# Windowed matmul on one core: row blocks of decreasing size, and PSUM sums added several banks at a time

## The chip, the cores and the metric

The kernel runs on one core of a Trainium2 chip. The metric is the device time of one execution in microseconds (us); the median of ten executions before the change is 182.23 us (181.94 to 182.52).

## The reference

```
B, S, D, W = 4, 4096, 4096, 64
x: [B, S, D] float32    w: [D, D] float32    offsets: [B] int64
for b in range(B):
    o = int(offsets[b])
    results.append(x[b, o:o+W] @ w)
return np.stack(results)          # [4, 64, 4096] float32
```

Four windows of 64 rows are cut out of x at offsets that are known only at run time, and each is multiplied by the same matrix w. Put together, the windows are 256 rows, so the work is one product of 256 x 4096 by 4096 x 4096. The matrix w is 67 MB of float32 and is read once.

## The kernel before

**Tiles.** The 256 rows are two groups g of 128 rows (two windows each). The contraction runs over 32 k tiles of 128 rows of w. The 4096 output columns are eight pieces c of 512, and two halves ng of 2048: the left half is ng = 0, the right one ng = 1. For each k tile there are 2 x 8 matmuls of 128x512, 512 in all. A matmul's stationary operand is a 128x128 piece of the transposed x, its moving operand 512 columns of w in fp16, and its output one PSUM bank of 512 float32. PSUM has eight banks (`ps[0]` to `ps[7]`, L54). Sums over k are kept in PSUM within a block and added to `acc[g]` in SBUF (float32, 128x4096 for each group) after it.

**Weights.** All of w but the first k tile comes by transfers that POOL issues and that convert float32 to fp16 on the way. K tiles 0 and 1 have tiles of their own. From k tile 2 on, `blocks` (L35) lists a first k tile and r, the number of rows of w that each partition takes: one transfer per block, r x 16 KB of source per partition in one run (L87 to L94). A block of r rows per partition covers r k tiles, and which rows of w belong to which k tile follows the stride r; `x_cols` (L120) picks the matching columns of x. K tiles 24 to 31 are the tail (`k_tail`, L36): they are loaded by column halves, the right half first (`order = [1, 0]`), in transfers of two k tiles by 2048 columns (1 MB as fp16), the last ones of the left half smaller (L97 to L118).

**Buffers.** Blocks and tail use one pool of three buffers, each of 4 x 4096 fp16 per partition (L42). There are eight uses: six blocks, the right half of the tail, the left half of the tail. The fourth use waits until the first is read, and so on. POOL issues in program order, so each transfer waits for the one before it and for its buffer.

**Order of the work.** The order is written out by hand (`manual_schedule`, L56): every engine takes its instructions in the order of the program. First come the transposes of x (L127 to L141), then k tiles 0 and 1, whose sums are copied to `acc` (L169, L171). Then come the blocks in `whole_rows` (L158): for each group and each column piece, one bank takes the r matmuls of the block, and VectorE adds the bank to `acc` (`add_out`, L154). The bank number goes round all eight. The last block (k tiles 21 to 23) is treated in two parts. Its left half goes through `whole_rows` (L178). Its right half is summed in the same PSUM banks as the tail's right half: L193 to L196 run over 11 k tiles on the outside, the two groups and the four column pieces on the inside, so that all eight banks (4 g + j) are open at once. After that VectorE adds two banks of each group, ScalarE copies the other two to `tmp` (L200), VectorE adds `tmp` (L205), and POOL issues the store of the right half of each group (L206, 1 MB each). At last comes the left half of the tail: k tiles 24 to 29 for all eight banks, then k tiles 30 and 31 for two column pieces of each group and then for the other two (L215 to L220). VectorE adds each bank, and the store of each group and each 1024 columns is issued on ScalarE's queue for group 0 and on SyncE's for group 1 (L225).

Of the kernel before, what the change touches and what calls it, by code (L numbers as in the profile page):

```python
# [10 lines left out]
def kernel(  # L11
# [7 lines left out]
    nc = tc.nc  # L19
    fp32 = mybir.dt.float32  # L20
    fp16 = mybir.dt.float16

    B, S, D = x.shape
    _, N = w.shape
    WIN = out.shape[1]
    P = 128
    NT = 512
    NG = N // 2
    n_k = D // P
    n_sub = NG // NT  # L30
    G = B // 2
    POOL = mybir.EngineType.Pool


    blocks = [(0, 1), (1, 1), (2, 4), (6, 4), (10, 4), (14, 4), (18, 3), (21, 3)]  # L35
    k_tail = 24  # L36
    n_fine = 2
    R_MAX = 4

# [2 lines left out]
    wc_pool = ctx.enter_context(tc.tile_pool(name="wc", bufs=3))  # L42
    w1_pool = ctx.enter_context(tc.tile_pool(name="w1", bufs=1))
    acc_pool = ctx.enter_context(tc.tile_pool(name="acc", bufs=1))
    psum_pool = ctx.enter_context(tc.tile_pool(name="ps", bufs=1, space=bass.MemoryType.PSUM))
# [3 lines left out]
    x16 = [x_pool.tile([P, D], fp16, name=f"xrow{g}") for g in range(G)]  # L49
    xT = [x_pool.tile([P, D], fp16, name=f"xT{g}") for g in range(G)]  # L50
    w_one = [w1_pool.tile([P, N], fp16, name=f"w1_{i}") for i in range(2)]
    tmp = [acc_pool.tile([P, NT], fp32, name=f"tmp{i}") for i in range(4)]
    acc = [acc_pool.tile([P, N], fp32, name=f"acc{g}") for g in range(G)]
    ps = [psum_pool.tile([P, NT], fp32, name=f"bank{t}") for t in range(8)]  # L54

    ctx.enter_context(tc.manual_schedule())  # L56

# [10 lines left out]
    for b in range(B):  # L68
        g, m = divmod(b, 2)
# [8 lines left out]
            out=x16[g][m * WIN : (m + 1) * WIN, :],  # L78
            in_=x[b][bass.ds(o, WIN), :],
# [3 lines left out]
    src = {  # L83
        0: lambda a, e: w_one[0][:, a:e],
        1: lambda a, e: w_one[1][:, a:e],
    }
    for k0, r in blocks[2:]:  # L87
        t = wc_pool.tile([P, R_MAX * N], fp16, name="wc", tag="wc")
        nc.gpsimd.dma_start(  # L89
            out=t[:, : r * N],  # L90
            in_=w[k0 * P : (k0 + r) * P, :].rearrange("(p r) n -> p (r n)", r=r),
        )
        for q in range(r):
            src[k0 + q] = lambda a, e, t=t, c=q * N: t[:, c + a : c + e]  # L94


    tail = {}  # L97
    order = [1, 0]
    steps = [(ki, 2, 0, NG) for ki in range(k_tail, n_k, 2)]
    fine_steps = steps[: -(n_fine // 2)]  # L100
    fine_steps.append((n_k - n_fine, n_fine, 0, NG // 2))
    fine_steps += [(ki, 1, NG // 2, NG) for ki in range(n_k - n_fine, n_k)]
    for ng, st in zip(order, (steps, fine_steps)):
        t = wc_pool.tile([P, R_MAX * N], fp16, name="wc", tag="wc")
        pos = 0
        for ki, n, c0, c1 in st:
            wd = c1 - c0
            nc.gpsimd.dma_start(  # L108
                out=t[:, pos : pos + n * wd].rearrange("p (t n) -> p t n", t=n),
                in_=w[ki * P : (ki + n) * P, ng * NG + c0 : ng * NG + c1].rearrange(  # L110
                    "(t p) n -> p t n", p=P
                ),
            )
            for q in range(n):
                for j in range(wd // NT):
                    a = pos + q * wd + j * NT
                    tail[(ki + q, (ng * NG + c0) // NT + j)] = t[:, a : a + NT]
            pos += n * wd  # L118

    def x_cols(g, kt):  # L120
        for k0, r in blocks:
            if k0 <= kt < k0 + r:
                a = k0 * P + kt - k0
                return x16[g][:, a : a + r * (P - 1) + 1 : r]
        return x16[g][:, kt * P : (kt + 1) * P]

    for g in range(G):  # L127
        for t in range(8):
            for i in range(4):
                nc.tensor.matmul(  # L130
                    out=ps[t][:, i * P : (i + 1) * P],
                    lhsT=x_cols(g, 4 * t + i),
                    rhs=identity[:],
                    start=True,
                    stop=True,
                )
            dst = xT[g][:, t * NT : (t + 1) * NT]
            if t % 2 == 0:
                nc.vector.tensor_copy(out=dst, in_=ps[t][:])  # L139
            else:  # L140
                nc.scalar.copy(out=dst, in_=ps[t][:])  # L141

    def mm(bank, g, kt, rhs, start, stop):
        nc.tensor.matmul(  # L144
            out=ps[bank][:],
            lhsT=xT[g][:, kt * P : (kt + 1) * P],
            rhs=rhs,
            start=start,
            stop=stop,
        )  # L150

    def add_out(bank, g, c):
        dst = acc[g][:, c * NT : (c + 1) * NT]
        nc.vector.tensor_add(out=dst, in0=dst, in1=ps[bank][:])  # L154

    n_bank = 0

    def whole_rows(kts, cols, first):  # L158
        nonlocal n_bank
        for g in range(G):  # L160
            for c in cols:
                bank = n_bank % 8
                n_bank += 1
                for i, kt in enumerate(kts):
                    mm(bank, g, kt, src[kt](c * NT, (c + 1) * NT), i == 0, i == len(kts) - 1)
                if not first:
                    add_out(bank, g, c)
                elif c % 2 == 0:
                    nc.vector.tensor_copy(out=acc[g][:, c * NT : (c + 1) * NT], in_=ps[bank][:])  # L169
                else:  # L170
                    nc.scalar.copy(out=acc[g][:, c * NT : (c + 1) * NT], in_=ps[bank][:])  # L171

    whole_rows([0, 1], range(8), True)
    for k0, r in blocks[2:-1]:
        whole_rows(range(k0, k0 + r), range(8), False)
    k0, r = blocks[-1]
    last_block = range(k0, k0 + r)
    whole_rows(last_block, range(order[1] * n_sub, (order[1] + 1) * n_sub), False)  # L178

    def tail_mm(ki, g, ng, j, start, stop):  # L180
        c = ng * n_sub + j
        rhs = src[ki](c * NT, (c + 1) * NT) if ki < k_tail else tail[(ki, c)]
        mm(4 * g + j, g, ki, rhs, start, stop)
# [3 lines left out]
    def store(eng, g, c0, c1, cuts=(0, P)):  # L187
        for a, e in zip(cuts, cuts[1:]):
            eng.dma_start(out=out_rows[g * P + a : g * P + e, c0:c1], in_=acc[g][a:e, c0:c1])  # L189

    ng = order[0]
    kts = list(last_block) + list(range(k_tail, n_k))
    for ki in kts:  # L193
        for g in range(G):
            for j in range(n_sub):
                tail_mm(ki, g, ng, j, ki == kts[0], ki == kts[-1])  # L196
    for g in range(G):
        for j in range(0, n_sub, 2):
            add_out(4 * g + j, g, ng * n_sub + j)
            nc.scalar.copy(out=tmp[2 * g + j // 2][:], in_=ps[4 * g + j + 1][:])  # L200
    for g in range(G):
        for j in range(1, n_sub, 2):
            c = ng * n_sub + j
            dst = acc[g][:, c * NT : (c + 1) * NT]
            nc.vector.tensor_add(out=dst, in0=dst, in1=tmp[2 * g + j // 2][:])  # L205
        store(nc.gpsimd, g, ng * NG, (ng + 1) * NG)  # L206

    ng = order[1]
# [5 lines left out]
    q = [nc.scalar, nc.sync]  # L214
    for h in range(2):  # L215
        js = range(h * n_sub // 2, (h + 1) * n_sub // 2)
        for ki in range(k_fine, n_k):
            for g in range(G):
                for j in js:
                    tail_mm(ki, g, ng, j, False, ki == n_k - 1)  # L220
        for g in range(G):
            for j in js:
                add_out(4 * g + j, g, ng * n_sub + j)
            c0 = ng * NG + h * NG // 2
            store(q[g], g, c0, c0 + NG // 2)  # L225

# [29 lines left out]
```

## Time and profile before

| what | value |
| --- | --- |
| median of ten executions | 182.23 us (181.94 to 182.52) |
| profiled execution, its time | 182.19 us |
| profiled execution, its span | 180.4 us |
| mean granted TensorE clock | 0.912 |
| PE busy | 126.0 us (70%), 576 matmuls |
| VectorE busy | 80.1 us (44%) |
| ScalarE, POOL busy | 16.2 us, 14.5 us |
| weight and store transfers issued by POOL | 36.70 MB, 93.9% of the 16 DMA engines' span |
| read from HBM, written to HBM | 71.30 MB, 4.19 MB |

The profile is of one execution. Its span is the time from the first to the last recorded event, and the execution's own time is 1.8 us more. PE is TensorE (PEld its weight loads), DVE is VectorE, ACT is ScalarE, POOL is GpSimd, SP is SyncE; L154 is line 154 of the kernel. Sizes of transfers are counted as they are written, so the weights count half of what is read for them. The rows by slice cut the span into 40 equal parts of 4.5 us and give the busy share of each in tenths. The chain of waits is followed back from the last instruction to what released it. In a row of a group the first number after the bar is its total busy time in us, the second the mean of one in ns, and behind the next bar stands the idle time of the engine ahead of it and what ended most of it.

### The profile page before, as it was taken

The numbers are of one execution on the slowest core, as the hardware profiler recorded it, in microseconds if no ns is written. First come the engines' busy times: TensorE is split into PE (matmuls) and PEld (weight loads), VectorE is DVE, ScalarE is ACT, GpSimd is POOL, SyncE is SP. The second block draws the span as 40 slices with busy tenths as digits, with TensorE's granted clock in tenths as the row PEclk, the third lists the DMA queues.
The fourth block names the chain that finished last, engine by engine and source line by source line (L and its number), as shares of the span: only waits on it lengthen the run. The fifth ranks groups of instructions, "written<-read, shape, count | busy, mean of one in ns | idle before, by whom it ended". The sixth has DMA issues, their size and how long they took to land.

```text
span 180.4 us, 1505 instructions
## 1 busy us (share of the span) xinstructions
PE 126.0 (70%) x576; PEld 57.0 (32%) x576; DVE 80.1 (44%) x120; ACT 16.2 (9%) x23; POOL 14.5 (8%) x29
## 2 busy tenths in 40 slices
PE   0000789104999199938998599999299999997900
PEld 0000754001444034402443144444134444443400
DVE  0000678100777147831687168899365000640460
ACT  2412556200000000000000000000000000400000
POOL 4600000000000100010001000050501100020000
PEclk9999999955899969985899699999969999999995
DMA  5999979999998899999989989898899999999995
GB/s 182 320 254 214 287 167 203 236 233 225 233 233 189 174 225 233 234 222 233 203 182 211 251 185 251 189 245 191 182 214 217 215 212 214 216 215 206 368 417 206
DMA packets 4952, 40.98 MB, mean 227 GB/s; under 512 B 466, under 2 KB 466, under 8 KB 3282
## 3 DMA queue, kind: packets, MB, share of 16 engines
q0 software_dynamic: 4080, 36.70, 93.9%
q1 hardware_dynamic: 432, 2.10, 3.1%
q10 hardware_dynamic: 434, 2.10, 2.9%
q8 instruction: 4, 0.07, 0.1%
q14 instruction: 2, 0.02, 0.0%
HBM read 71.30 MB, written 4.19 MB: 419 GB/s over the span
## 4 chain that ended last, share of the span: by engine, by line
DMA 63%; PE 26%; issue 3%; DVE 2%; POOL 1%; POOLq 1%; DVEq 0%
DMA wc<-in_w_dram 63%; PE bank L144 26%; DVE acc L154 2%; POOL wc L108 1%; POOLq L70 1%; POOL xrow L77 0%; DVEq L251 0%; POOL identity masks.py:197 0%; POOLq L77 0%; POOL w L66 0%; POOLq masks.py:199 0%; DVEq L154 0%; POOLq L240 0%
## 5 line engine op out<-in xcount | busy, mean ns | idle before, releaser
L144 PE MATMUL bank<-wc,xT 128*128 128x512 f16 x480 | 113.6, 401 | 25.9 <-DMA wc<-in_w_dram 25.9
L154 DVE TENSOR_TENSOR acc<-acc,bank 128x512 f32<-128x512 f32 x100 | 67.1, 687 | 72.2 <-PE bank L144 71.4
L144 PEld LDWEIGHTS <-xT 128*128 128x128 f16 x512 | 51.9, 102 | 94.2 <-DMA wc<-in_w_dram 27.0
L130 PE MATMUL bank<-identity,xrow 128*128 128x128 f16 x64 | 5.5, 264 | 19.8 <-DMA xrow<-in_x_dram 19.8
L139 DVE CAST xT<-bank 128x512 f16<-128x512 f32 x8 | 5.3, 687 | 21.0 <-PE bank L130 21.0
L200 ACT COPY tmp<-bank 128x512 f32<-128x512 f32 x4 | 2.1, 600 | 122.2 <-PE bank L144 122.2
L130 PEld LDWEIGHTS <-xrow 128*128 128x128 f16 x64 | 5.1, 125 | 20.0 <-issue 20.0
L89 POOL DMA_DIRECT2D wc<-in_w_dram x6 | 3.2, 542 | 89.2 <-PE bank L144 89.2
L108 POOL DMA_DIRECT2D wc<-in_w_dram x10 | 6.7, 683 | 34.9 <-PE bank L144 25.3
L144 PE MATMUL bank<-w,xT 128*128 128x512 f16 x32 | 7.1, 379 | 0.0
L169 DVE COPY acc<-bank 128x512 f32<-128x512 f32 x8 | 5.4, 689 | 0.9 <-PE bank L144 0.6
L141 ACT CAST xT<-bank 128x512 f16<-128x512 f32 x8 | 4.4, 592 | 7.1 <-PE bank L130 7.1
L171 ACT COPY acc<-bank 128x512 f32<-128x512 f32 x8 | 4.7, 585 | 2.1 <-PE bank L144 2.1
L189 POOL DMA_DIRECT2D out_dram<-acc x2 | 1.1, 534 | 18.6 <-DVE acc L205 18.6
L205 DVE TENSOR_TENSOR acc<-acc,tmp 128x512 f32<-128x512 f32 x4 | 2.5, 684 | 0.0
L63 ACT CAST w<-acc 128x2048 f16<-128x2048 f32 x1 | 1.9, 1897 | 4.8 <-DMA acc<-in_w_dram 4.8
L77 POOL DMA_DIRECT2D xrow<-in_x_dram x4 | 2.1, 523 | 2.1 <-issue 2.1
L62 ACT CAST w<-acc 128x2048 f16<-128x2048 f32 x1 | 1.9, 1897 | 2.9 <-DMA acc<-in_w_dram 2.9
L62 ACT ACT_TABLE_LOAD x1 | 1.3, 1283 | 1.8 <-PEq L240 1.8
L66 POOL DMA_DIRECT2D w<-in_w_dram x1 | 0.7, 660 | 0.8 <-POOLq L240 0.8
masks.py:199 POOL TENSOR_SCALAR_AFFINE_SELECT identity<-identity 128x128 f16<-128x128 f16 x1 | 0.3, 287 | 0.1
masks.py:197 POOL MEMSET identity<- 128x128 f16 x1 | 0.2, 223 | 0.0
(4 smaller groups left out, 0.4 us busy)
## 6 DMA issues: line engine op xcount, KB each, us to landing
wc<-in_w_dram POOLq DMA_DIRECT2D x4, 4096.0 KB, 48.7
wc<-in_w_dram POOLq DMA_DIRECT2D x7, 1024.0 KB, 27.4
wc<-in_w_dram POOLq DMA_DIRECT2D x2, 3072.0 KB, 34.4
xrow<-in_x_dram POOLq DMA_DIRECT2D x4, 512.0 KB, 14.5
out_dram<-acc POOLq DMA_DIRECT2D x2, 1024.0 KB, 13.9
acc<-in_w_dram SPq DMA_DIRECT2D x1, 1024.0 KB, 5.1
w<-in_w_dram POOLq DMA_DIRECT2D x1, 1024.0 KB, 12.0
acc<-in_w_dram ACTq DMA_DIRECT2D x1, 1024.0 KB, 11.3
```

Of the source, the lines that this page charges most:

```text
L62: nc.scalar.copy(out=w_one[0][:, :NG], in_=w0_32[:, :NG])
L77: nc.gpsimd.dma_start(out=x16[g][m * WIN : (m + 1) * WIN, :], in_=x[b][bass.ds(o, WIN), :],)
L89: nc.gpsimd.dma_start(out=t[:, : r * N], in_=w[k0 * P : (k0 + r) * P, :].rearrange("(p r) n -> p (r n)", r=r),)
L108: nc.gpsimd.dma_start(out=t[:, pos : pos + n * wd].rearrange("p (t n) -> p t n", t=n), in_=w[ki * P : (ki + n) * P, ng * NG + c0 : ng * NG ...
L130: nc.tensor.matmul(out=ps[t][:, i * P : (i + 1) * P], lhsT=x_cols(g, 4 * t + i), rhs=identity[:], start=True, stop=True,)
L139: nc.vector.tensor_copy(out=dst, in_=ps[t][:])
L141: nc.scalar.copy(out=dst, in_=ps[t][:])
L144: nc.tensor.matmul(out=ps[bank][:], lhsT=xT[g][:, kt * P : (kt + 1) * P], rhs=rhs, start=start, stop=stop,)
L154: nc.vector.tensor_add(out=dst, in0=dst, in1=ps[bank][:])
L169: nc.vector.tensor_copy(out=acc[g][:, c * NT : (c + 1) * NT], in_=ps[bank][:])
L171: nc.scalar.copy(out=acc[g][:, c * NT : (c + 1) * NT], in_=ps[bank][:])
L205: nc.vector.tensor_add(out=dst, in0=dst, in1=tmp[2 * g + j // 2][:])
```

## The change

It has two parts.

**Blocks.** The list ends in blocks of 4, 3, 2 and 1 rows per partition, where it ended in 3 and 3. The last two blocks (k tiles 25, 26 and 27, `n_join = 2`) are summed together. Blocks share a buffer where it has room: the block of 2 and that of 1 lie in one. The tail is k tiles 28 to 31, and its two halves lie in one buffer. The uses of the three buffers are thus: five blocks of four, the block of 3, the joined blocks, the tail.

**Sums.** PSUM is held as two tiles of four banks (`quads`). In `whole_rows` PE fills four banks and VectorE adds all four to `acc` in one instruction of 2048 columns; the first copies are 2048 wide as well. The joined blocks' left half and the right half with the tail both go through a new function `columns`, k tiles outermost and eight banks open: VectorE adds two banks of each group in one instruction, ScalarE copies the other two to `tmp` in one, and VectorE adds `tmp` in one. The last adds of the left half take two banks each.

```diff
-    blocks = [(0, 1), (1, 1), (2, 4), (6, 4), (10, 4), (14, 4), (18, 3), (21, 3)]
-    k_tail = 24
+    blocks = [(0, 1), (1, 1), (2, 4), (6, 4), (10, 4), (14, 4), (18, 4), (22, 3), (25, 2), (27, 1)]
+    n_join = 2
+    k_tail = 28
...
-    tmp = [acc_pool.tile([P, NT], fp32, name=f"tmp{i}") for i in range(4)]
+    tmp = [acc_pool.tile([P, 2 * NT], fp32, name=f"tmp{i}") for i in range(G)]
...
-    ps = [psum_pool.tile([P, NT], fp32, name=f"bank{t}") for t in range(8)]
+    quads = [psum_pool.tile([P, 4 * NT], fp32, name=f"banks{t}") for t in range(2)]
+
+    def banks(b, n=1):
+        return quads[b // 4][:, b % 4 * NT : (b % 4 + n) * NT]
...
+    free = 0
     for k0, r in blocks[2:]:
-        t = wc_pool.tile([P, R_MAX * N], fp16, name="wc", tag="wc")
+        if free < r:
+            t = wc_pool.tile([P, R_MAX * N], fp16, name="wc", tag="wc")
+            free = R_MAX
+        base = (R_MAX - free) * N
+        free -= r
         nc.gpsimd.dma_start(
-            out=t[:, : r * N],
+            out=t[:, base : base + r * N],
             in_=w[k0 * P : (k0 + r) * P, :].rearrange("(p r) n -> p (r n)", r=r),
         )
...
+    t = wc_pool.tile([P, R_MAX * N], fp16, name="wc", tag="wc")
+    pos = 0
     for ng, st in zip(order, (steps, fine_steps)):
-        t = wc_pool.tile([P, R_MAX * N], fp16, name="wc", tag="wc")
-        pos = 0
...
+    def add_out(bank, n, g, c):
+        dst = acc[g][:, c * NT : (c + n) * NT]
+        nc.vector.tensor_add(out=dst, in0=dst, in1=banks(bank, n))
+
+    n_quad = 0
+
+    def whole_rows(kts, first=False):
+        nonlocal n_quad
+        for g in range(G):
+            for c in range(0, 2 * n_sub, 4):
+                b0 = n_quad % 2 * 4
+                n_quad += 1
+                for j in range(4):
+                    for i, kt in enumerate(kts):
+                        rhs = src[kt]((c + j) * NT, (c + j + 1) * NT)
+                        mm(b0 + j, g, kt, rhs, i == 0, i == len(kts) - 1)
                 if not first:
-                    add_out(bank, g, c)
...
+                    add_out(b0, 4, g, c)
+                elif c == 0:
+                    nc.vector.tensor_copy(out=acc[g][:, :NG], in_=banks(b0, 4))
                 else:
-                    nc.scalar.copy(out=acc[g][:, c * NT : (c + 1) * NT], in_=ps[bank][:])
-
-    whole_rows([0, 1], range(8), True)
-    for k0, r in blocks[2:-1]:
-        whole_rows(range(k0, k0 + r), range(8), False)
...
+                    nc.scalar.copy(out=acc[g][:, NG:], in_=banks(b0, 4))
+
+    whole_rows([0, 1], True)
+    for k0, r in blocks[2:-n_join]:
+        whole_rows(range(k0, k0 + r))
+    join = range(blocks[-n_join][0], k_tail)
...
+    def columns(ng, kts):
+        for ki in kts:
+            for g in range(G):
+                for j in range(n_sub):
+                    tail_mm(ki, g, ng, j, ki == kts[0], ki == kts[-1])
+        for g in range(G):
+            add_out(4 * g, 2, g, ng * n_sub)
+            nc.scalar.copy(out=tmp[g][:], in_=banks(4 * g + 2, 2))
+        for g in range(G):
+            c = ng * n_sub + 2
+            dst = acc[g][:, c * NT : (c + 2) * NT]
+            nc.vector.tensor_add(out=dst, in0=dst, in1=tmp[g][:])
+
+    columns(order[1], list(join))
     ng = order[0]
...
+    columns(ng, list(join) + list(range(k_tail, n_k)))
     for g in range(G):
...
         store(nc.gpsimd, g, ng * NG, (ng + 1) * NG)
...
         for g in range(G):
-            for j in js:
-                add_out(4 * g + j, g, ng * n_sub + j)
+            add_out(4 * g + js[0], 2, g, ng * n_sub + js[0])
             c0 = ng * NG + h * NG // 2
             store(q[g], g, c0, c0 + NG // 2)
```

More of the change, by code (lines that the diff above doesn't have):

```diff
@@ L93 @@
         for q in range(r):
-            src[k0 + q] = lambda a, e, t=t, c=q * N: t[:, c + a : c + e]
+            src[k0 + q] = lambda a, e, t=t, c=base + q * N: t[:, c + a : c + e]
     tail = {}
@@ L130 @@
                 nc.tensor.matmul(
-                    out=ps[t][:, i * P : (i + 1) * P],
+                    out=banks(t)[:, i * P : (i + 1) * P],
                     lhsT=x_cols(g, 4 * t + i),
@@ L138 @@
             if t % 2 == 0:
-                nc.vector.tensor_copy(out=dst, in_=ps[t][:])
+                nc.vector.tensor_copy(out=dst, in_=banks(t))
             else:
-                nc.scalar.copy(out=dst, in_=ps[t][:])
+                nc.scalar.copy(out=dst, in_=banks(t))
     def mm(bank, g, kt, rhs, start, stop):
         nc.tensor.matmul(
-            out=ps[bank][:],
+            out=banks(bank),
             lhsT=xT[g][:, kt * P : (kt + 1) * P],
@@ L150, in mm @@
         )
[L152 to L159, printed above, removed]
-        for g in range(G):
[L161 to L165, printed above, removed]
+    def add_out(bank, n, g, c):
[4 more added lines that the diff above has]
+        nonlocal n_quad
+        for g in range(G):
+            for c in range(0, 2 * n_sub, 4):
[5 more added lines that the diff above has]
+                        mm(b0 + j, g, kt, rhs, i == 0, i == len(kts) - 1)
                 if not first:
-                    add_out(bank, g, c)
-                elif c % 2 == 0:
-                    nc.vector.tensor_copy(out=acc[g][:, c * NT : (c + 1) * NT], in_=ps[bank][:])
-                else:
-                    nc.scalar.copy(out=acc[g][:, c * NT : (c + 1) * NT], in_=ps[bank][:])
-    whole_rows([0, 1], range(8), True)
-    for k0, r in blocks[2:-1]:
-        whole_rows(range(k0, k0 + r), range(8), False)
-    k0, r = blocks[-1]
-    last_block = range(k0, k0 + r)
-    whole_rows(last_block, range(order[1] * n_sub, (order[1] + 1) * n_sub), False)
+                    add_out(b0, 4, g, c)
+                elif c == 0:
+                    nc.vector.tensor_copy(out=acc[g][:, :NG], in_=banks(b0, 4))
+                else:
+                    nc.scalar.copy(out=acc[g][:, NG:], in_=banks(b0, 4))
[3 more added lines that the diff above has]
+    join = range(blocks[-n_join][0], k_tail)
     def tail_mm(ki, g, ng, j, start, stop):
@@ L189, in store @@
             eng.dma_start(out=out_rows[g * P + a : g * P + e, c0:c1], in_=acc[g][a:e, c0:c1])
-    ng = order[0]
[L192 to L196, printed above, removed]
-    for g in range(G):
-        for j in range(0, n_sub, 2):
-            add_out(4 * g + j, g, ng * n_sub + j)
[L200 to L205, printed above, removed]
+    def columns(ng, kts):
[11 more added lines that the diff above has]
+    columns(order[1], list(join))
+    ng = order[0]
+    columns(ng, list(join) + list(range(k_tail, n_k)))
+    for g in range(G):
         store(nc.gpsimd, g, ng * NG, (ng + 1) * NG)
@@ L221 @@
         for g in range(G):
-            for j in js:
-                add_out(4 * g + j, g, ng * n_sub + j)
+            add_out(4 * g + js[0], 2, g, ng * n_sub + js[0])
             c0 = ng * NG + h * NG // 2
```

## The prediction

> **What bounds the kernel now.** I read the slices first, then the chain, then each transfer's issue and landing, then the last 17 us in steps of one us.
>
> ```profile
> PE   0000789104999199938998599999299999997900
> DVE  0000678100777147831687168899365000640460
> DMA  5999979999998899999989989898899999999995
> ```
>
> The DMA row is at 8 or 9 tenths nearly throughout. PE and DVE show gaps in the first two thirds; from slice 22 (about 100 us) PE has almost none.
>
> ```profile
> 101.28 25.77 PE bank L144 x112
> 127.05 0.29 issue
> 127.34 1.39 POOL wc L108 x2
> 128.73 35.86 DMA wc<-in_w_dram
> 164.59 0.04 issue
> 164.63 5.35 PE bank L144 x24
> 169.98 1.35 DVE acc L154 x3
> ```
>
> The chain is read from the bottom: last adds, last matmuls, a weight transfer that had been queued for 36 us. A long queue means that the transfers, not their issue, set the pace. Adding each issue time to its time to landing gives the landings (us): k tiles 2-5 at 43.0, 6-9 at 62.3, 10-13 at 81.8, 14-17 at 101.3, 18-20 at 115.8, 21-23 at 130.1; then the tail pieces of 1 MB at 135.1, 140.1, 144.9, 149.9 (right half) and 154.7, 159.7, 164.6 (left), and the small ones at about 167.1, 168.3 and 169.6. So 4 MB blocks come every 19.45 us (4.86 us per MB) and tail pieces every 4.92 us. The queue is never empty: the weights land as fast as they can.
>
> ```profile
> L154 DVE TENSOR_TENSOR acc<-acc,bank 128x512 f32<-128x512 f32 x100 | 67.1, 687 | 72.2 <-PE bank L144 71.4
> L200 ACT COPY tmp<-bank 128x512 f32<-128x512 f32 x4 | 2.1, 600 | 122.2 <-PE bank L144 122.2
> ```
>
> A bank's add takes 687 ns, its copy on ACT 600. In the timeline eight adds back to back take 4.87 us, so they overlap to 0.61 us each.
>
> ```profile
> 167.00:168.00 1.00, 1.00 (x6) 0.49 (x5) 0.00 (x0) 0.00 (x0) 0.00 (x0) 1.00 1.18 256
> 168.00:169.00 1.00, 1.00 (x7) 0.45 (x5) 0.00 (x0) 0.00 (x0) 0.00 (x0) 1.00 1.02 358
> 169.00:170.00 1.00, 1.00 (x6) 0.43 (x5) 0.64 (x2) 0.00 (x0) 0.00 (x0) 1.00 1.05 438
> ...
> 177.00:178.00 1.00, 0.00 (x0) 0.00 (x0) 0.00 (x0) 0.00 (x0) 0.00 (x0) 0.50 0.87 356
> ```
>
> These are stretches of one us; the last two columns are DMA share and GB/s. Weights are written as halves, so they count about 213 GB/s; outputs count about 420. The rise from 213 to 438 shows the weights' last bytes at about 168.1, and 4.2 MB of output following **without a gap** until about 178.1 (the 356 is the drain). This works because the right half's two 1 MB stores were issued on POOL at 158.8 and 159.96 and stood in the queue behind the weights. The PE side ends at nearly the same time: the last 32 matmuls wait for the 164.6 landing and end at 171.7, the adds at 174.23, and the last store is issued at 174.3. DMA and PE are thus both near the end; slack between them is about 1.3 us (PE is idle from 163.35 to 164.63).
>
> [...] after waits of 3.2 to 3.8 us some 8 matmuls or more start 0.43 us apart, after that of 1.28 us none do (32 in 7.07 us). [...]
>
> **The change part by part.**
>
> *Blocks and tiles.* Matmuls stay at 512 plus the transposes, weight bytes are the same, and there are still eight uses of three buffers. POOL's weight issues fall from 16 to 14; all are hidden behind a queue of over 10 us. Blocks: k tiles 18-21 (E) land at 101.3 + 19.45 = 120.7; 22-24 (F) at 135.1; 25-26 at 144.8; 27 at 149.7; right tail pieces at 154.6 and 159.5; left ones at 164.4, 166.9, 168.1, 169.4. The tail's buffer waits for the matmuls of E, over at 136.5, when 13 us of transfers are still queued: no gap. Moving 4 MB from 1 MB pieces to blocks saves 4 x 0.06 = 0.24 us at the last landing. That is all the DMA can gain.
>
> *Wide adds in the blocks.* A four-bank add costs 2.29 us ([...]four single adds in a row, 2.48 us, bound it from above[...]). PE fills four banks in 16 x 0.216 = 3.46 us with 4 rows and 12 x 0.216 = 2.59 with 3 rows (0.216: 105 matmuls from 130.22 to 154.65, less the slow start). DVE keeps up, barely, for F. In the first pass (two rows, 1.73 us a fill) PE waits a little; the arrival at 43.0 covers it, and without that cover it would cost about 0.6 us.
>
> *From F to the join.* This is the new wait that I price highest. Before, PE went round eight single banks. Now F's last four banks are one add that starts when F's last matmul ends. The join runs k outermost, so its fifth matmul needs bank 4. PE issues four matmuls (0.86 us) and stands until 2.29 + 0.1 us after F's end: **1.5 us of stall** (0 if something else is later; 1.7 with the upper price). Everything later on PE is queued behind it.
>
> *Two column changes* (left join to right, right to left tail). Before, j0's bank came free after one 0.69 us add. Now two banks wait for one 1.22 us add (1.15 to 1.24), and group 1's add stands behind group 0's on DVE; ACT copies two banks in about 1.03 us (twice 0.60 at most). Group 0's first bank comes free about when PE wants it (0.05 late), group 1's about 0.3 later than wanted: 0.35 us each, 0.7 in all (0.2 to 1.2). In the trace of before, I see no such wait at 156.
>
> *PE's sum from E.* E starts at 120.75 and takes 15.8 (mean of 15.46, 15.67, 16.54 and 15.4 of the four-row blocks): 136.55. F: 48 x 0.216 = 10.4, 146.9. Join left: 0.86, the stall to 149.35, 20 more = 4.3, 153.7 (k tile 27 landed at 149.7, before it is wanted). Right half: 0.35 + 56 x 0.216 = 12.1, 166.15 (its last weights have been there since 159.5). Left tail: 0.35 + 32 x 0.216 = 6.9: **173.4, against 171.7**. The PE has more to do late than before, because E is now a full block that comes 4.9 us later than the three-row one did, and no wait for weights is left to absorb the stalls.
>
> *Final adds.* Four of 1.15 us (overlapped as before) from the tenth matmul before the end, 173.4 - 2.15 = 171.25: 175.9 against 174.23. Wide or narrow makes no difference here (4.6 against 4.87 with a start 0.2 us later). So the last store is issued 1.7 later.
>
> *The right half's stores.* They hang on the copies and adds after 166.15: DVE add g0 from 164.9 to 166.1, g1 to 167.25, tmp adds to 168.4 and 169.55. POOL issues at 168.7 and 169.9 instead of 158.8 and 159.96. They no longer stand behind weights: the weights' last bytes are at 167.9[...]. The DMA **idles 1.8 to 2.3 us**, and 4.2 MB take 10.05 us as before: last byte at 180.0 against 178.1, so +1.9. The last store (+1.7) and the DMA (+1.9) nearly coincide and don't add up.
>
> *Sum.* 180.4 + 1.9 = 182.3 of span. The profiled execution took 182.19, 1.8 more than its span and 0.04 under the median of 182.23. 182.3 + 1.8 = 184.1.
>
> **The rivals.**
> 1. As above, stalls and late stores: 184.1 (183.2 to 184.9 with the bounds: smaller or larger changes of columns[...]). Chance 0.63.
> 2. The 1.5 us stall, or waits near it, lets the clock fall: 8 matmuls at 0.43 instead of 0.216 add 1.7 us, or E's slow start is longer: 185.8. For it: 3.2 us was enough. Against: 1.28 us was not. Chance 0.18.
> 3. The stall is covered, because F's or k tile 27's weights come later than I have them or the adds release banks earlier: PE ends at 171.8, the right half's stores are issued near 167, the idle is a few tenths: 182.2 to 182.4, no change. Against it: 149.35 is close to 149.7, but the join's first k tiles are there at 144.8. Chance 0.09.
> 4. Faster: the DMA, which in the trace dips to 147 and 102 GB/s between 127 and 129 us, where POOL turns from blocks to tail pieces, keeps its 213 through a smoother sequence of sizes. The price is (2 x 213 - 249)/213 = 0.8 us, with the 0.24 above: up to 1.0 us, 181.2. It decides only if PE ends before about 170.7, that is, if all stalls and 1 us of E's start vanish; the landings on both sides of that dip show no gap. Chance 0.10.
>
> That the change doesn't do what it says (waits kept for whole four-bank tiles rather than banks, so that the last half waits for the adds of the half before) lies in case 2: some 2 us more.
>
> **How the numbers follow.** The likeliest case gives 184.1. The range leaves out about 2 in 10: 182.2 (case 3's lower end) to 185.9 (case 2 and its clock). 0.2% is 0.36 us, about what a measurement of this kernel can tell from no change: faster is case 4 (0.10), same is case 3 (0.09), slower the rest (0.81).
>
> **What would show it.** Right: a PE wait for DVE of about 1.5 us near 147, POOL's stores issued near 168.7, a DMA gap of about 2 us near 168 to 170, last adds near 175.9, L154 at about 2.29 us for 2048 elements. Wrong: the buffer of the tail coming free after 149 (the weights would then land late, and every number shifts), PE waiting for weights after 160, or stores still queued behind weights.

## The result and the profile after

The changed kernel takes 185.58 us (median of nine runs, 185.27 to 186.75) against 182.32 us (31 runs); the ratio is 1.0184, 95% interval 1.0173 to 1.0195: 3.3 us slower. The profiled execution took 185.15 us with a span of 183.3, against 182.19 and 180.4. Traces are compared by their spans: +2.9 us.

The slices of the changed kernel, each of 4.6 us:

```profile
PE   0000444499999599619992999179999966996940
DVE  0000333335177445710775176404678837207371
DMA  5999999889999999899999999899899999997695
```

Its chain of waits over the last 35 us, in order of time (start, length, what):

```profile
139.87 6.27 PE banks L154 x29
...
146.16 2.30 DVE acc L164
...
148.50 3.63 PE banks L154 x16
...
153.29 1.23 DVE acc L164
154.52 0.02 issue
154.54 1.02 ACT tmp L208
...
155.61 10.53 PE banks L154 x48
...
167.30 1.22 DVE acc L164
...
168.60 1.02 ACT tmp L208
...
174.89 1.23 DVE acc L164
176.11 0.04 issue
176.16 1.04 PE banks L154 x4
```

Before, this stretch was one weight transfer of 36 us and then PE; PE itself ran on through the changes of columns without a wait:

```profile
134.56 28.80 PE L144 MATMUL bank<-wc,xT 128*128 128x512 f16 x131
```

Now no transfer is in the chain: PE is followed by DVE, DVE by ACT, ACT by PE again. PE is waiting for sums to be carried out of PSUM. The groups that do it:

```profile
L164 DVE TENSOR_TENSOR acc<-acc,banks 128x2048 f32<-128x2048 f32 (+1 forms) x32 | 64.3, 2021 | 64.1 <-PE banks L154 64.1
L208 ACT COPY tmp<-banks 128x1024 f32<-128x1024 f32 x4 | 4.0, 1012 | 117.5 <-DVE acc L164 117.2
```

VectorE is less busy with its adds than before (64.3 us against 67.1; the mean mixes 2048 and 1024 columns). What is new is the end of the second line: ACT's copies waited for **DVE**, where they had waited for PE. The copy reads banks 2 and 3 of a group and the add reads banks 0 and 1. They share no bank, only the four-bank tile. The matmuls of the timeline show the same (start, length, [idle before, and what ended it]):

```profile
148.50 4.48 PE L154 MATMUL banks<-wc,xT 128*128 128x512 f16 x20 [1.51 <-DVE acc L164]
154.47 5.83 PE L154 MATMUL banks<-wc,xT 128*128 128x512 f16 x25 [1.49 <-ACT tmp L208]
168.54 5.61 PE L154 MATMUL banks<-wc,xT 128*128 128x512 f16 x24 [1.55 <-ACT tmp L208]
175.03 0.59 PE L154 MATMUL banks<-wc,xT 128*128 128x512 f16 x2 [0.88 <-DVE acc L164]
176.16 1.46 PE L154 MATMUL banks<-wc,xT 128*128 128x512 f16 x6 [0.54 <-DVE acc L164]
```

The first is the wait between block F and the join. The second and third are the two changes of columns: the matmul wants bank 0, free since DVE's add, and waits for ACT's copy of banks 2 and 3. At each change another 0.39 us follows at the second group (PE's weight loads stop until 155.61 and 169.67). The last two stand ahead of the last quarter: it writes banks 2 and 3 of each group, while DVE adds banks 0 and 1. In all 1.51 + 1.49 + 0.39 + 1.55 + 0.39 + 0.88 + 0.54 = 6.75 us.

The effect on the DMA, in stretches of one us (after the length come the busy times of PE, PEld, DVE, ACT and POOL, then the granted TensorE clock, the DMA share and GB/s):

```profile
167.00:168.00 1.00, 0.00 (x0) 0.00 (x0) 1.00 (x2) 0.53 (x1) 0.00 (x0) 1.00 0.80 148
168.00:169.00 1.00, 0.46 (x3) 0.22 (x3) 1.00 (x2) 0.88 (x2) 0.00 (x0) 1.00 0.21 39
169.00:170.00 1.00, 0.89 (x5) 0.35 (x4) 1.00 (x2) 0.62 (x1) 0.00 (x0) 1.00 0.00 0
170.00:171.00 1.00, 1.00 (x7) 0.43 (x5) 0.88 (x1) 0.00 (x0) 0.54 (x1) 1.00 0.00 0
171.00:172.00 1.00, 1.00 (x6) 0.45 (x5) 0.00 (x0) 0.00 (x0) 0.53 (x1) 1.00 0.94 393
```

At the full 213 GB/s the weights would end at 167 + (148 + 39)/213 = 167.9; their last bytes trickle in until nearly 169. The right half's stores are issued at 170.04 and 171.17, and the first byte moves at about 171.1. Counted so, **the DMA loses about 3.2 us**. The last adds end at 179.57 (174.23 before), the last store is issued at 179.6 and lands in 2.8 us (5.2 before, behind a backlog).

### The profile page after: what moved, and what is told of

Read it like the earlier page. It is cut to its first block, busy times and chain, and to the rows that moved or that the text cites. A ratio compares the mean times of both kernels' runs of the same rounds, so it can differ in the third digit from the quotient of the medians.

```text
span 183.3 us, 1367 instructions
## 1 busy us (share of the span) xinstructions
PE 127.2 (69%) x576; PEld 57.7 (31%) x576; DVE 79.1 (43%) x46; ACT 17.5 (10%) x17; POOL 12.7 (7%) x27
## 4 chain that ended last, share of the span: by engine, by line
PE 49%; DMA 31%; DVE 8%; issue 5%; ACT 2%; DVEq 1%; another core or an unknown queue 1%; POOLq 0%; POOL 0%; ACTq 0%
PE banks L154 44%; DMA wc<-in_w_dram 24%; DMA xrow<-in_x_dram 7%; PE banks L140 5%; DVE acc L164 3%; DVE xT L149 3%; ACT xT L151 1%; DVE acc L181 1%; ACT tmp L208 1%; DVEq L262 1%; POOLq L75 0%; POOL identity masks.py:197 0%; POOL xrow L82 0%; POOLq L82 0%
## 5 line engine op out<-in xcount | busy, mean ns | idle before, releaser
L154 PE MATMUL banks<-wc,xT 128*128 128x512 f16 x480 | 108.8, 387 | 22.7 <-DMA wc<-in_w_dram 16.2
L164 DVE TENSOR_TENSOR acc<-acc,banks 128x2048 f32<-128x2048 f32 (+1 forms) x32 | 64.3, 2021 | 64.1 <-PE banks L154 64.1
L140 PE MATMUL banks<-identity,xrow 128*128 128x128 f16 x64 | 8.9, 302 | 27.5 <-DMA xrow<-in_x_dram 18.3
L149 DVE CAST xT<-banks 128x512 f16<-128x512 f32 x8 | 5.5, 692 | 30.2 <-PE banks L140 30.2
L208 ACT COPY tmp<-banks 128x1024 f32<-128x1024 f32 x4 | 4.0, 1012 | 117.5 <-DVE acc L164 117.2
L154 PE MATMUL banks<-w,xT 128*128 128x512 f16 x32 | 9.8, 470 | 0.2 <-ACT acc L183 0.2
L181 DVE COPY acc<-banks 128x2048 f32<-128x2048 f32 x2 | 4.6, 2292 | 6.1 <-PE banks L154 6.1
L151 ACT CAST xT<-banks 128x512 f16<-128x512 f32 x8 | 4.7, 585 | 17.3 <-PE banks L140 17.3
L212 DVE TENSOR_TENSOR acc<-acc,tmp 128x1024 f32<-128x1024 f32 x4 | 4.7, 1222 | 0.0
L183 ACT COPY acc<-banks 128x2048 f32<-128x2048 f32 x2 | 3.7, 1866 | 7.3 <-PE banks L154 7.3
```

The lines of the kernel that those rows point to most:

```text
L140: nc.tensor.matmul(out=banks(t)[:, i * P : (i + 1) * P], lhsT=x_cols(g, 4 * t + i), rhs=identity[:], start=True, stop=True,)
L149: nc.vector.tensor_copy(out=dst, in_=banks(t))
L151: nc.scalar.copy(out=dst, in_=banks(t))
L154: nc.tensor.matmul(out=banks(bank), lhsT=xT[g][:, kt * P : (kt + 1) * P], rhs=rhs, start=start, stop=stop,)
L164: nc.vector.tensor_add(out=dst, in0=dst, in1=banks(bank, n))
L181: nc.vector.tensor_copy(out=acc[g][:, :NG], in_=banks(b0, 4))
```

## The experiments

Two accounts had to be told apart. **Theory P**: PE waits for whole four-bank tiles, so its work, the right half and the last adds come late. **Theory R**: what is paid for is the gap in the DMA behind the weights. P can be the cause of R's gap; but each may also set the end by itself. The rivals were Q (the blocks load PE late, whatever the sums) and W (long adds hold banks too long). Each median is given with that of the kernel before on the same chip. The ratio is taken over the runs of both, with its 95% interval; where the times scatter it is not quite that of the medians.

### Blocks alone, and sums alone

Blocks alone: `blocks`, buffers and tail of the change; eight one-bank tiles, and `whole_rows`, adds and copies of the kernel before (against the changed kernel).

```diff
...
-    columns(order[1], list(join))
+    whole_rows(join, range(order[1] * n_sub, (order[1] + 1) * n_sub), False)
...
```

> The new blocks with the sums of the kernel before (eight tiles of one bank, one-bank adds and copies). Theory P (the time is lost because PE waits for a whole four-bank tile, whichever of its banks it wants): no PE wait for DVE or ACT, PE ends at 170.5 to 171.7, right half's stores issued near 167, 182.0 to 182.7 us. Rival Q (the blocks themselves, since a full block now comes late and loads PE late): PE ends after 174, 184 us or more.

Measured: 184.63 us (before 182.44), ratio 1.0128 (1.0095 to 1.0161); three of its six runs took 183.8 to 183.9 us and three 185.3 to 185.6, and the trace is of one of the first. That looks like Q, but the trace says otherwise:

```profile
149.70 23.90 PE L154 MATMUL bank<-wc,xT 128*128 128x512 f16 x110 [2.61 <-DMA wc<-in_w_dram]
```

PE waited for no adder. It waited 2.61 us for k tile 27, since bank by bank the first bank needs all three joined k tiles, and the right half's stores were issued at 169.21. Expectation and rival both missed this: my edit had undone the k-outermost order of the join as well. A second version keeps it, still with eight one-bank tiles and one-bank adds and copies:

```diff
-    whole_rows(join, range(order[1] * n_sub, (order[1] + 1) * n_sub), False)
+    columns(order[1], list(join))
```

> The new blocks with eight tiles of one bank and one-bank adds, the joined blocks summed with k outermost on the left half too, as in the changed kernel. Theory P (the new sums' waits make the right half late): no PE wait for DVE or ACT, the right half's stores issued near 167, no DMA gap over 0.5 us, 182.0 to 182.7 us. Rival Q (the blocks themselves): like the run with blocks alone, 184 us or more.

Measured: **182.05 us (before 182.28), ratio 0.9988 (0.9981 to 0.9994)**. PE has only one wait that the profile puts down to an adder, of 0.45 us at 164.47, where its weight load was waiting for the DMA. The right stores are issued at 166.52 and 167.73, and the DMA has no gap. Q is out: the blocks by themselves cost nothing, and bring 0.2 us.

Sums alone: the new sums with the blocks of before (each half of the tail has its own buffer again).

```diff
-    blocks = [(0, 1), (1, 1), (2, 4), (6, 4), (10, 4), (14, 4), (18, 4), (22, 3), (25, 2), (27, 1)]
-    n_join = 2
-    k_tail = 28
+    blocks = [(0, 1), (1, 1), (2, 4), (6, 4), (10, 4), (14, 4), (18, 3), (21, 3)]
+    n_join = 1
+    k_tail = 24
...
```

> The old blocks with the new sums (two tiles of four banks, wide adds). Theory P: the waits of 1.5 us and more stand at each change of columns and at the last quarter; the right half's stores are still issued while weights are queued, so there is no DMA gap, but the last adds end near 177: 183 to 184 us. Rival Q: 182.1 to 182.6 us.

Measured: 182.6 us (182.32 to 184.75; before 182.44), ratio 1.0027 (1.0006 to 1.0047); the profiled execution, at 183.36, is among its longer ones. The waits at the columns and at the last quarter are all there, 1.49 and 1.55 us and then 0.88 and 0.54, and the last adds end at 177.63, 3.4 us late. But the right half's stores were issued at 161.2 and 162.33, with weights still in the queue, and there was no gap behind the weights. So P's waits alone cost 0.3% here, less than I expected. The last adds have slack in the kernel before, since its last store waits behind a backlog in any case. Here the backlog had run out before the last stores came, and the DMA stood still in part:

```profile
173.00:174.00 1.00, 0.59 (x2) 0.19 (x2) 1.00 (x2) 0.00 (x0) 0.00 (x0) 1.00 0.33 135
176.00:177.00 1.00, 0.00 (x0) 0.00 (x0) 1.00 (x2) 0.00 (x0) 0.00 (x0) 1.00 0.53 209
177.00:178.00 1.00, 0.00 (x0) 0.00 (x0) 0.64 (x1) 0.00 (x0) 0.00 (x0) 1.00 0.63 258
```

The last store thus landed in 2.7 us and not in 5.2. The slack is 2.4 us (the run of the kernel before without its right stores, below), and 3.4 - 2.4 = 1.0 us is what the span of this execution grew by (181.4 against 180.4). **The two parts together cost more (1.84%) than one by one (-0.12% and +0.27%).**

### Tile size against width of the adds

Pairs: the changed kernel with four tiles of two banks, and adds and copies of 1024 columns. At the changes of columns the adds and copies are 1024 wide in both kernels, so only the tile differs there.

```diff
-    quads = [psum_pool.tile([P, 4 * NT], fp32, name=f"banks{t}") for t in range(2)]
+    pairs = [psum_pool.tile([P, 2 * NT], fp32, name=f"banks{t}") for t in range(4)]
...
-        nc.vector.tensor_add(out=dst, in0=dst, in1=banks(bank, n))
+        for i in range(0, n, 2):
+            dst = acc[g][:, (c + i) * NT : (c + i + 2) * NT]
+            nc.vector.tensor_add(out=dst, in0=dst, in1=banks(bank + i, 2))
...
```

> The changed kernel with four tiles of two banks and adds of 1024 columns everywhere. Theory P: ACT's copies no longer wait for DVE's adds, PE waits 0.3 to 0.4 us at a change of columns and not at the last quarter, PE ends near 171.5, 182.0 to 182.7 us. Rival W (the width of the adds itself costs the time, since a bank comes free only when a long add ends): about half of the loss remains, 183.5 to 184.5 us.

Measured: 182.31 us (before 182.44), ratio 1.0 (0.9989 to 1.0011): the whole loss is gone. In the timeline the copies no longer wait for the adds:

```profile
151.15 1.93 ACT L213 COPY tmp<-banks 128x1024 f32<-128x1024 f32 x2 [108.30 <-PE banks L154]
```

The wait is for PE again, and 0.43 us after DVE's first add has begun. PE runs on through the changes of columns with pauses of 0.30 to 0.47 us in its weight loads (the longest ends with a transfer of weights), and the right stores are issued at 167.03.

Narrow adds in the four-bank tiles: the tiles of the change, each add and copy of one bank.

```diff
-        nc.vector.tensor_add(out=dst, in0=dst, in1=banks(bank, n))
+        for i in range(n):
+            dst = acc[g][:, (c + i) * NT : (c + i + 1) * NT]
+            nc.vector.tensor_add(out=dst, in0=dst, in1=banks(bank + i))
...
```

> The changed kernel with its two four-bank tiles, but every add and copy of one bank (four in a row where there was one). Theory P: the waits stay, a little longer since four adds take 2.46 us and not 2.29: 185.5 to 186.5 us. Rival W: most of the loss goes, 182.3 to 183.5 us.

Measured: 187.78 us (before 182.44), ratio 1.0276 (1.0254 to 1.0299), more than P expected. W is out: narrow adds in four-bank tiles win nothing back. That the kernel is even about 2 us slower than the changed one is mostly another thing. In this execution block E (k tiles 18 to 21) starts more slowly; here is the same stretch of both, the changed kernel first (the third column from the right is the granted clock):

```profile
124.00:126.00 2.00, 2.00 (x11) 0.93 (x10) 0.55 (x1) 0.00 (x0) 0.00 (x0) 1.00 1.03 221
124.00:126.00 2.00, 2.00 (x6) 0.76 (x5) 0.00 (x0) 0.00 (x0) 0.00 (x0) 0.50 0.91 197
```

The first add of E thus begins at 127.08 and not at 125.45, 1.6 us late, before any narrow add of E has run. From there to the first right store (172.54 against 170.04) another 0.9 us is lost, and that is what narrow adds can have cost. Whether the other runs of this kernel had the slow start is not shown. Its DMA stands still for some 5 us.

### The order of the matmuls against the tiles

The last quarter by groups: the last two k tiles for group 0, then for group 1.

```diff
-    for h in range(2):
-        js = range(h * n_sub // 2, (h + 1) * n_sub // 2)
+    for g in range(G):
         for ki in range(k_fine, n_k):
-            for g in range(G):
-                for j in js:
+            for j in range(n_sub):
```

> The changed kernel with its last two k tiles done for group 0, then for group 1 (in place of first two and last two column pieces of both), so that PE never wants a four-bank tile while it is added. Theory P: the PE waits of 0.88 and 0.54 us go and the last adds end 1.2 us earlier, near 178.4; theory R: as the DMA starts the stores no earlier, only the 0.5 us that it starves between 178 and 180 us is won: 184.8 to 185.3 us. P alone would give 184.2 to 184.5.

Measured: 185.25 us (before 182.28), ratio 1.0161 (1.0145 to 1.0176). The waits of 0.88 and 0.54 us are gone, yet the last adds end at 179.3, not 178.4 (this execution ran 0.5 us late from 149 on, and both of a group's adds wait for its eight last matmuls). The DMA gap stays, and so does nearly all of the time: from the first byte of the right stores at about 171.6 to its end near 182 the DMA now has no hole, so here the gap sets the end.

Grouped throughout: tiles and adds of the change; the joined blocks and the tail in chunks, each for group 0 and then for group 1, and each group's `tmp` add directly behind its first add.

```diff
-    columns(order[1], list(join))
+    columns(order[1], [[25], [26, 27]])
...
-    columns(ng, list(join) + list(range(k_tail, n_k)))
+    columns(ng, [[25, 26, 27], [28], [29, 30, 31]])
...
+    for g, kts, js in [(0, [28, 29], range(4)), (0, [30, 31], range(2)), (1, [28, 29], range(4)),
+                       (0, [30, 31], range(2, 4)), (1, [30, 31], range(4))]:
...
```

> The changed kernel with its tiles and wide adds as they are, but with the matmuls of the joined blocks and the tail ordered so that one group's four banks get several k tiles before the other group's do, and each group's tmp add directly behind its first add. Theory P (PE's waits for whole four-bank tiles make it late): the waits at the end fall from 6.7 to about 3 us, the last adds end near 176, the first right store is issued near 166.6 and the gap in the DMA shrinks to 0.5 us: 182.7 to 183.6 us. Rival (what is lost has another cause than the order of the matmuls against the tiles): 185 us or more.

Measured: 183.73 us (before 182.39), ratio 1.0072 (1.0055 to 1.0089), 0.1 above what P gave. The waits fall to 1.51 + 0.63 + 0.68 + 0.72 = 3.54 us, the last adds end at 177.46. The first right store comes at 168.08, not at 166.6, so the gap behind the weights shrinks to 1.1 us only. A second one, of about 1.0 us, follows: the second right store is issued at 171.57, when the first has just been written.

```profile
171.00:172.00 1.00, 1.00 (x6) 0.42 (x5) 0.27 (x1) 0.00 (x0) 0.43 (x1) 1.00 0.64 262
172.00:173.00 1.00, 1.00 (x6) 0.49 (x5) 0.15 (x1) 0.00 (x0) 0.10 (x1) 1.00 0.43 180
```

With tiles and widths untouched, over half of the loss goes with the order of matmuls and adds alone.

### What sets the end: the last adds or the gap

Without the right half's stores (that half of the output is missing, but for four columns), the changed kernel and the kernel before (the edit of the first; in the second the same line is replaced):

```diff
-    for g in range(G):
-        store(nc.gpsimd, g, ng * NG, (ng + 1) * NG)
+    store(nc.gpsimd, 0, ng * NG, ng * NG + 4)
```

> The changed kernel without the right half's stores (only a sliver of 4 columns is written, so the right half of the output is missing). If the last adds set the end (theory P alone), it stays at 184.8 to 185.5 us; if the DMA backlog behind the gap sets it (theory R), it falls by 2 us or more, to 183.5 or less.

Measured: 185.65 us (before 182.28), ratio 1.0198 (1.0172 to 1.0224): nothing gained by leaving out 2 MB. The last adds of the changed kernel set its end by themselves.

> The kernel before without the right half's stores (only a sliver of 4 columns is written, so the right half of the output is missing). If the DMA sets its end (theory R), the last store lands some 2.7 us after its issue at 174.3 and not 5.2: 179.2 to 180.2 us. If the last adds set it: 182 us.

Measured: 179.83 us (182.28 with them), ratio 0.987 (0.9855 to 0.9885): 2.4 us gained. The end of the kernel before is set by the DMA and not by its adds, which end at 174.1 and 174.23. Its last adds could thus come 2.4 us later and cost nothing.

Late stores: the kernel before, its right half's stores held back on POOL until the first add of the end.

```diff
-        store(nc.gpsimd, g, ng * NG, (ng + 1) * NG)
...
+        if h == 0:
+            late = const_pool.tile([1, 1], fp32, name="late")
+            nc.gpsimd.tensor_copy(out=late[:], in_=acc[0][0:1, c0 : c0 + 1])
+            for g in range(G):
+                store(nc.gpsimd, g, order[0] * NG, (order[0] + 1) * NG)
```

> The kernel before with the right half's stores held back on POOL until the first add of the left half's end (a copy of one element on POOL, ahead of the stores, waits for it), so that they are issued near 170.3 and not at 158.8; matmuls, adds and the last four stores are as before. Theory R (a DMA gap behind the weights costs its own length): a gap of about 3 us, 184.8 to 185.5 us, with the last adds still near 174.2. Rival (only the last adds set the end): 182.2 to 182.6 us.

Measured: 185.2 us (before 182.39), ratio 1.0143 (1.0126 to 1.016), span 183.3. Its stretches of one us:

```profile
168.00:169.00 1.00, 1.00 (x7) 0.42 (x5) 0.00 (x0) 0.00 (x0) 0.00 (x0) 1.00 0.29 53
169.00:170.00 1.00, 1.00 (x6) 0.47 (x5) 0.39 (x1) 0.00 (x0) 0.00 (x0) 1.00 0.04 6
170.00:171.00 1.00, 1.00 (x6) 0.47 (x5) 1.00 (x3) 0.00 (x0) 0.58 (x2) 1.00 0.00 0
171.00:172.00 1.00, 0.94 (x5) 0.21 (x3) 1.00 (x2) 0.00 (x0) 0.66 (x2) 1.00 0.32 131
```

The weights end at 168.1 and the stores begin at about 171.7: a gap of some 3.5 us, with PE and the adds where they were (the last add ends at 174.5). The span grows by 2.9 us. So a gap behind the weights costs most of its own length, with no help from late adds.

**What follows.** With these blocks, P is the cause: the waits follow the tile and the order, and are there with wide adds and narrow ones, with new blocks and old. What they cost depends on the blocks: with the old ones the last adds lose their slack and little more (0.3%), with the new ones the right stores come too late as well. They then do harm in two ways at once, by the late adds and by the gap. The last adds are 5.3 us late, and less the slack of 2.4 that is 2.9, the growth of the span; a gap of some 3.5 us costs 2.9 by itself in the kernel before. As the two ways end so near each other, mending one alone wins little: without the right stores nothing is gained, and in the run with the last quarter by groups, where the adds end only 0.3 us earlier, 0.3 us.

What puts these waits there, the chip or the tools that build the program from its tiles, was not tried.

## Why the prediction was right, and where it was too small

The direction and the range (182.2 to 185.9) held, and so did the path: PE stalls behind block F, the right half's stores come behind the weights, the DMA stands idle. What makes PE wait at the columns was not in the likeliest case, and 184.1 was 1.5 us short, since it priced 1.9 us in place of 3.3. That 185.58 lies in the range is in part luck: the likeliest case ended at 184.9, and the range reached to 185.9 for a slower clock, which did not come (the mean granted clock is 0.966, against 0.912 before).

- *From F to the join*: 1.5 us forecast, 1.51 measured.
- *Two column changes*: forecast 0.35 us each, measured 1.49 + 0.39 and 1.55 + 0.39, 3.8 in all. **This is the term that was mis-sized**: it let bank 0 come free after the two-bank add, while PE waited for DVE's add and then ACT's copy, one after the other because they read one tile. "In the trace of before, I see no such wait at 156" was true and said nothing: there each bank was a tile.
- *Final adds*: the 1.42 us of waits ahead of the last quarter were not in the sum. They belong to the waits "for whole four-bank tiles" in rival 2, priced at some 2 us in all; these are 4.5 us of PE (3.1 beyond the forecast at the columns, 1.4 at the end). That part of the rival was right and belonged in the likeliest case.
- *PE's sum from E*: E began at 120.50 (forecast 120.75), F ended at 146.14 (146.9), so 0.8 us came back. The rise of PE's load through the blocks was harmless by itself, as the run with k outermost shows.
- *Final adds and last store*: the last add ended at 179.57 in place of 175.9, and 3.1 + 1.4 - 0.8 gives those 3.7 us. The sum also left out the 2.4 us of slack: its own last store, 1.7 us late, would have cost nothing, and its 1.9 us were those of the gap alone.
- *The right half's stores*: the weights' end at 167.9 was met, the issue was 170.04, not 168.7; the first byte came about 1.1 us later, and about 1.1 us again in the run with late stores (issue 170.59, first byte about 171.7). The trace of before does not show this time, as the stores found weights in the queue there; the forecast of the gap took a figure for it that was not shown. The gap was about 3.2 us and not 1.8 to 2.3.
- *Wide adds in the blocks*: hidden, as forecast: from 46.48 to 146.14 us PE waits for no add. An add took 2.29 us for 2048 columns (mean of 24) and 1.22 for 1024 (mean of 8), as the prediction had them. The trace of before, whose adds all have 512 columns, did not show these widths; it gave the bound of 2.48 us, the time of four in a row.
- *Slow starts* (rival 2's other half): after the waits of 1.5 us no matmul starts 0.43 us apart (20 in 4.48 us from 148.50), and the granted clock stays at 1.00. The prediction's "waits of 3.2 to 3.8 us" before slow starts leaves one out: at 101.28 the kernel before has one after 2.85 us, with a granted clock of 0.50 from 101 to 104. Rival 3's price (182.2 to 182.4) is what the run with pairs gives; rival 4's 1 us appears nowhere.

Not foreseen and harmless: at the start PE's transposes waited for the casts of other banks of their tile (18.3 to 36.4 us, against 18.3 to 25.1), so the first block began at 46.48 and not at 43.13. The queue of three blocks hid it, and E landed on time. It is the same wait as at the end, and was the plainest sign of it:

```profile
19.68 0.58 PE L140 MATMUL banks<-identity,xrow 128*128 128x128 f16 x4 [0.78 <-DVE xT L149]
```

Open: the times of the sums alone spread over 2.4 us (seven of 13 at 182.3 to 182.6, six at 183.2 or more), those of the kernel before over 0.5, and those of the blocks alone fall into two groups. What makes them spread was not tried. In the traced execution of the sums alone the 24 matmuls from 130.19 took 7.04 us, where 24 x 0.216 is 5.2. Whether such slow starts spread the times of the kernels whose end hangs on PE is not shown, as one execution of each has a trace.

## What to carry to other kernels

Where several PSUM banks are put into one tile for the sake of wide adds, look who else touches the other banks of that tile: here readers and writers of different banks waited for each other (6.75 us of PE's waits at the end), and two banks to a tile kept adds of 1024 columns without the waits (182.31 us). In a kernel bound by its transfers, as this one is, look whether a store is in the queue before the loads ahead of it run out: here a gap of some 3.5 us cost 2.9. Look also how much slack the last store has, since a delay costs only what goes beyond it. And ask of two edits what each takes from the other's slack: here each was within 0.3%, and the two together cost 1.8%.

## What the runs showed of the hardware that I had not expected

The weights (four k tiles of float32, 8.39 MB, per 19.45 us) were read at 431 GB/s by one core. After an idle PE the slow start of matmuls 0.43 us apart is not regular: it came after only 2.85 us (the kernel before, at 101.28, 64 matmuls in 15.4 us), and not after 3.49 us (the changed kernel, at 101.07, with a granted clock of 1.00 from 101 to 107, 64 matmuls in 13.99 us).
